# A two-layer hybrid trunk on one core: output stores and residual loads move from SyncE's queue to GpSimd's, and the sums of weights are issued earlier

## The chip, the core and the metric

The kernel runs on one core of a Trainium2 chip. The core has five engines that each work through a queue of their own: TensorE (PE, matrix products), VectorE (DVE), ScalarE (ACT), GpSimd (POOL) and SyncE (SP, which here only issues DMA transfers). ACT and GpSimd can issue DMA transfers too. Sixteen DMA engines move the data. The metric is the time of one execution in microseconds (us); less is better. A row of a view names the line of kernel.py (L115 is line 115), the engine, the operation and its operands by the program's names (out<-in).

## The reference

The input has 512 tokens of width 1024, to which 16 learned meta tokens are prepended, 528 positions in all. Two layers (DEPTH is 2) do the following, in fp32, and the meta positions are dropped at the end:

```python
for l in range(DEPTH):
    h = rmsnorm(h_res, norm_gain[l])
    proj = h @ w_in[l]
    u_pool, z_pool, c_q, c_kv, k_rope, z_mla, g_pool, g_mla = jnp.split(proj, IN_SPLIT_POINTS, axis=-1)
    y_pool = (pool_mix(u_pool, pool_w_group[l], pool_scale[l]) * jax.nn.silu(z_pool)) @ pool_w_up[l]
    o_mla = mla(c_q, c_kv, k_rope, pos, ...)
    y_mla = (o_mla * jax.nn.silu(z_mla)) @ mla_w_up[l]
    merged = jax.nn.sigmoid(g_pool) * y_pool + jax.nn.sigmoid(g_mla) * y_mla
    h_res = h_res + merged @ w_out[l]
```

`mla` is causal attention with 8 heads over low-rank queries and keys, with a norm on both; `pool_mix` takes running means over windows of 2, 4, 8 and 16 positions. The last line is the one that matters here: the product with `w_out` is added to the residual stream, which the next layer reads.

## The kernel before

All activations are held transposed, as tiles of 128 features by 528 positions, and each product works on the positions in two halves of 264 (in layer 1 mostly 256). An fp32 product is made of three products at reduced precision: weights and activations are split into a high and a low part, and `mm3` (lines 187 to 193) issues high by high (L188), high by low (L191) and low by high (L192) into one accumulator.

Weights come from DRAM in chunks of 128 by 512 (256 KB). `fetch` (L115) issues the load on SP's queue into one of three buffers named `raw`; ACT makes the high part `whi` (L183) and DVE the low part `wlo` (L184). Loads are requested four chunks ahead of their use, and a load can't start until `wlo` of the chunk three before it has been made, since that frees the buffer.

Two groups of products are done by a scheme that saves multiplications and needs sums of weight chunks instead: four output tiles of the product with `w_out` (m = 3 to 6, the tuple `OUT`) in each layer, with sums named `wsum`, and the gate tiles of layer 1, with sums named `wsumgp`. The sums are made in DRAM by transfers alone. `weight_sums` yields eight small functions for each pair of weight tiles: four copies, issued by SP (L350), and four adds, issued by GpSimd (L353), which accumulate onto the copies. An issue waits for a matmul that stands a given time back in the planner's count: `behind(ins, earlier(9000))` makes a copy wait for the last `mm3` that was planned 9000 ns or more before, and an add waits for one 4000 ns back.

What sets the order: the program is written by a planner that keeps a clock `clk` of estimated matmul time. `upto(name)` runs the plan of products until the named one is done; `after(ns, fn)` calls `fn` when the clock has moved on by `ns`. In layer 0 the functions of `weight_sums` are called every 4000 ns from a point behind the product `y3` (`up("y3")`), in layer 1 every 4500 ns. On top of this a scheduler of the language sets the final order on each engine; so the program's order on an engine isn't always the order of the code.

At the end of a layer the eight mu tiles (`mu0` to `mu7`, the products with `mla_w_up`) are made, then `blend` prepares the scheme's operands, and the output tiles follow: o0, o1, o2, the four of `OUT` (`out_pairs`), then o7. For the four of `OUT`, `residual` (L1098) loads the residual into `xb` on GpSimd's queue ahead of time, and `finish` adds to it in place and stores on GpSimd's queue: to the DRAM buffer `scr` in layer 0 (L1121), to the output `yT` in layer 1. For m = 0, 1, 2 and 7, `ev_o` does all of this on SP: it loads the residual into a temporary tile when the product is done (from `scr` in layer 1, L1060; from the input `xT` in layer 0, L1063), lets DVE add (L1066), and stores from SP (`yT` at L1070, `scr` at L1072). Between mu and out in layer 0, `meta_queries` and `meta_out` handle the attention of the meta positions; lines 1011, 1013, 1027 and 1028 belong to that, and line 297 is the split of an activation into its parts.

Of the kernel before, what the change touches and what calls it, by code (L numbers as in the profile page):

```python
# [14 lines left out]
ALU = mybir.AluOpType  # L15
# [7 lines left out]
NM = 16  # L23
# [35 lines left out]
OUT = (3, 4, 5, 6)  # L59
# [13 lines left out]
def trunk(ctx, tc, xT, pos, win, wkr, wqb, wkb, wvb, wgr, wpu, wmu, wout, gains, const, yT):  # L73
    nc = tc.nc
    pe, act, dve, gp, sp = nc.tensor, nc.scalar, nc.vector, nc.gpsimd, nc.sync
# [11 lines left out]
    def nm(s):  # L87
        uid[0] += 1
        return f"{s}_{uid[0]}"
# [4 lines left out]
    def tmp(w=W):  # L94
        return tp.tile([P, w], F32, tag="tmp", name=nm("tmp"), bufs=3)
# [15 lines left out]
    xb = cp.tile([P, 8, W], F32, name="xb")  # L111
# [30 lines left out]
    def other_loads(made):  # L142
        for k, m in ((2, 0), (4, 1), (6, None)):
            ins = sp.dma_start(xb[:, k:k + 2, :T], xT[:, k:k + 2, :])
            behind(ins, made)
            if m is not None:
                raw = rawt()
                behind(sp.dma_start(raw, win[0, MT_CKV + m, :, 512:1024]), made)
                early.append(raw)
        behind(sp.dma_start(cst, const), made)  # L150
        behind(sp.dma_start(posb[:, :T], pos.partition_broadcast(P)), made)
        dve.tensor_copy(maskw[:, 512 - P:], cst[:, C_MASK:C_MASK + P])
        dve.tensor_copy(identr, ident)
# [43 lines left out]
    def earlier(ns):  # L197
        return next((m for c, m in reversed(past) if c <= clk[0] - ns), past[0][1])
# [52 lines left out]
    def step():  # L251
        c = next(main, None)
        if c is None:
            flush()
            return False
        clk[0] += c
        while pend and pend[0][0] <= clk[0]:
            pend.pop(0)[1]()
        return True

    def after(ns, fn):
        pend.append((clk[0] + ns, fn))
        pend.sort(key=lambda e: e[0])

    def ready():
        while pend and pend[0][0] <= clk[0] + 12000.0:
            pend.pop(0)[1]()
# [5 lines left out]
    def upto(name):  # L273
        while name not in done:
            if not step():
                break
# [10 lines left out]
    def fill_now(ns):  # L287
        end = clk[0] + ns
        while clk[0] < end and step():
            pass  # L290
# [9 lines left out]
    def behind(ins, other):  # L300
        tc.add_manual_dep(ins.ins, other.ins.name,
                          mybir.DependencyInfo(mybir.DependencyClass.Sync, mybir.DependencyReason.DATA))
# [24 lines left out]
    scr = dp.tile([P, 8, SEQ], F32, name="scr")  # L327
# [13 lines left out]
    def weight_sums(name, w):  # L341
        def made(u, i):
            a, b = w[2 * u], w[2 * u + 1]
            d = wsum[name][u]
            src = {0: (b[:, 0:512], b[:, 512:1024]), 2: (a[:, 0:512], b[:, 0:512]), 1: (a[:, 0:512], d[:, 0, :]),
                   3: (a[:, 512:1024], d[:, 1, :])}
            return d[:, i, :], src[i]

        def copy(d, src):
            behind(sp.dma_start(d, src[0]), earlier(9000))  # L350

        def add(d, src):
            behind(gp.dma_start(d, src[1], accum_op=ALU.add), earlier(4000))  # L353

        for u in range(len(w) // 2):
            for fn, i in ((copy, 0), (copy, 2), (add, 0), (copy, 1), (add, 2), (add, 1), (copy, 3), (add, 3)):
                yield lambda fn=fn, u=u, i=i: fn(*made(u, i))

    class Layer:
# [695 lines left out]

        def ev_o(self, m, nxt):
            def ev(ps, a, b):
                xr = tmp()
                if self.last:
                    sp.dma_start(xr[:, a:b], scr[:, m, a - NM:b - NM])  # L1060
                    xn = xr
                else:
                    sp.dma_start(xr[:, a:b], xT[:, m, a:b])  # L1063
                    nxt.xt[m] = xb[:, m]
                    xn = nxt.xt[m]
                dve.scalar_tensor_tensor(out=xn[:, a:b], in0=ps, scalar=0.5, in1=xr[:, a:b],  # L1066
                                         op0=ALU.mult, op1=ALU.add)
                a0 = max(a, NM)
                if self.last:
                    sp.dma_start(yT[:, m, a - NM:b - NM], xn[:, a:b])  # L1070
                    return
                sp.dma_start(scr[:, m, a0 - NM:b - NM], xn[:, a0:b])  # L1072
                if m == 7:
                    nxt.square_x(m)
            return ev
# [168 lines left out]
        def go(self, nxt):  # L1244
            l = self.l
            up = lambda name: upto((l, name))
            mix = iter(range(99))
            if l == 0:
                for k in range(8):
                    if k in (0, 1, 3, 5):  # L1250
                        step()
                    self.split_h(k)
                    if k == 0:
                        other_loads(first)
            up("ckv1")
            if l == 0:
                for k in range(8):
                    self.square_x(k)
            self.norm_sums()
            up("u1")  # L1260
            for m in range(2):
                self.mix(m, self.window(m))
            up("u3")
            s2 = self.window(2)
            up("k3")
            s3 = self.window(3)
            up("zp0")
            self.mix(2, s2)
            up("zp1")
            self.mix(3, s3)  # L1270
            self.k_factors()
            up("y3")
            if l == 0:
                sums = [*weight_sums(0, [wout[0, m] for m in OUT]), *weight_sums("gp", [win[1, MT_GP + m] for m in range(8)])]
                for i, fn in enumerate(sums):
                    after(4000 * (i + 1), fn)
            up("qr1")
            for s, (a, b) in enumerate(FULL):
                a0 = max(a, self.x0)
                self.stat(self.acc[:, a0:b], a0, b, C_CQ, self.acc_last)  # L1280
            up("qn3")
            self.qk_stats()
            if l == 0:
                fill_now(2600)
            kq = self.prep(0)
            if l == 1:
                for i, fn in enumerate(weight_sums(1, [wout[1, m] for m in OUT])):
                    after(4500 * (i + 1), fn)
            fill_now(2600)
            due[0] = None  # L1290
            prev = None
            for h in range(H):
                kn_ = self.head(h, kq, prev, lambda: self.mixed(next(mix)))
                self.gap()
                self.mixed(next(mix))
                if h + 1 < H:
                    kq = self.prep(h + 1)
                self.pv(prev, (2, 3))
                prev = kn_
                self.gap()  # L1300
                self.mixed(next(mix))
            fill_now(1300)
            self.pv(prev, (0, 1))
            fill_now(2600)
            if not self.last:
                self.meta_queries()
            self.pv(prev, (2, 3))
            up("gm6")
            if self.last:
                self.gates_again()  # L1310
            up("gm7")
            ready()
            if not self.last:
                for p in range(4):
                    self.meta_out(p)
            up("mu7")
            for m in OUT:
                self.residual(m)
            for k in range(4):
                fill_now(2600)  # L1320
                self.blend(k)
            up("o7")
            if nxt is not None:
                for k in range(8):
                    nxt.split_h(k)
# [76 lines left out]
```

## Time and profile before

| what | before |
|---|---|
| median of the runs (lowest, highest) | 789.2 us (788.14, 790.12) |
| the profiled execution's own time | 790.13 us |
| its span, first to last instruction | 788.4 us |
| mean granted TensorE clock in it | 0.998 |
| PE busy | 776.1 us, 98% |
| DVE busy | 592.9 us, 75% |
| ACT busy | 442.5 us, 56% |
| GpSimd busy | 212.4 us, 27% |
| moved by DMA | 109.15 MB, mean 138 GB/s |

Of the DMA engines' time, SP's queue takes 39.6% of the span (q1 in the profile) and GpSimd's 9.5% (q0). A load of a `raw` chunk lands some 3 us after its issue in the median. "Busy" counts time in which an engine works on an instruction; issuing a DMA counts on GpSimd (0.5 to 0.9 us each), and is shown on SP as its queue (SPq). In a list of waits, "PE mm L188 <- ACT q L297: 1.9, 1, 1.9" reads: PE's instructions of line 188 stood for 1.9 us in total, once, 1.9 us at most, until ACT's instruction of line 297 that wrote q had finished. The granted clock is the share of full TensorE speed that the chip allowed in a stretch.

### The profile page before, as it was taken

How to read it: one execution, taken by the hardware profiler on the slowest of the kernel's cores; microseconds unless marked ns; L12 is line 12 of the kernel's file. 1: busy time of each engine (PE TensorE's matmuls, PEld its weight loads, DVE VectorE, ACT ScalarE, POOL GpSimd, SP SyncE). 2: the span in 40 equal slices, each digit the busy share in tenths (PEclk: the TensorE clock that was granted, in tenths of full speed). 3: DMA queues.
4: the chain of work that ended last, by engine and by line, in shares of the span. 5: the costliest groups of instructions: out<-in, count | busy, mean ns of one | idle time of the engine just before them, and what ended most of it. 6: DMA issues, size and time to landing. Idle time of an engine off the chain costs nothing.

```text
span 788.4 us, 15369 instructions
## 1 busy us (share of the span) xinstructions
PE 776.1 (98%) x5493; PEld 713.6 (91%) x5493; DVE 592.9 (75%) x1329; ACT 442.5 (56%) x1007; POOL 212.4 (27%) x291
## 2 busy tenths in 40 slices
PE   8999999999999999999999999999999999999998
PEld 8999899999999999899997898887788899888888
DVE  5847788447779987589875487775998899874995
ACT  7645656635656565544564356555657676754451
POOL 1034504103343352101110145131015325440101
PEclk9999999999999999999999999999999999999999
DMA  6242334764556355658732422435356566664552
GB/s 242 81 101 83 99 120 130 180 161 129 132 139 140 102 129 154 137 166 191 224 122 93 96 87 80 133 94 167 114 146 150 165 169 168 156 208 133 163 173 81
DMA packets 65196, 109.15 MB, mean 138 GB/s; under 512 B 10448, under 2 KB 16976, under 8 KB 65120
## 3 DMA queue, kind: packets, MB, share of 16 engines
q1 hardware_dynamic: 58096, 93.72, 39.6%
q0 software_dynamic: 6016, 12.62, 9.5%
q10 hardware_dynamic: 1008, 1.84, 0.6%
q8 instruction: 43, 0.70, 0.4%
q14 instruction: 33, 0.27, 0.1%
HBM read 100.18 MB, written 22.62 MB: 156 GB/s over the span
## 4 chain that ended last, share of the span: by engine, by line
PE 89%; DMA 4%; DVE 3%; issue 2%; ACT 2%; POOL 0%; ACTq 0%; DVEq 0%; POOLq 0%
PE mm L188 26%; PE mm L192 26%; PE mm L191 25%; PE mm L946 2%; PE S L191 2%; PE S L188 2%; PE S L192 2%; DMA raw<-win 1%; DVE wlo L184 1%; PE o L952 1%; PE o L951 1%; DMA raw<-wout 1%; PE S L500 1%; ACT whi L183 1%; DMA xb<-xT 1%
## 5 line engine op out<-in xcount | busy, mean ns | idle before, releaser
L188 PE MATMUL mm<-hh,whi 128*128 128x264 f32 (+2 forms) x1000 | 306.9, 310 | 1.0 <-DVE u L543 0.3
L191 PE MATMUL mm<-hl,whi 128*128 128x264 f32 (+2 forms) x1000 | 305.4, 307 | 0.0
L192 PE MATMUL mm<-hh,wlo 128*128 128x264 f32 (+2 forms) x1000 | 304.9, 308 | 0.2 <-DVE wlo L184 0.2
L184 DVE TENSOR_TENSOR wlo<-raw,whi 128x512 fp32r<-128x512 f32 (+2 forms) x261 | 188.6, 727 | 98.5 <-ACT whi L183 91.6
L183 ACT ACTIVATE whi<-raw 128x512 fp32r<-128x512 f32 (+2 forms) x261 | 156.3, 602 | 164.4 <-PE mm L191 83.5
L188 PEld LDWEIGHTS mm<-hh,whi 128*128 128x128 f32 x1000 | 187.5, 188 | 12.2 <-ACT whi L183 1.4
L191 PEld LDWEIGHTS mm<-hl,whi 128*128 128x128 f32 x1000 | 188.1, 188 | 8.7
L192 PEld LDWEIGHTS mm<-hh,wlo 128*128 128x128 f32 x1000 | 187.2, 188 | 8.9 <-DVE wlo L184 0.8
L188 PE MATMUL mm<-cq,whi 128*128 128x264 f32 (+2 forms) x156 | 48.6, 312 | 0.9 <-ACT whi L183 0.9
L192 PE MATMUL mm<-cq,wlo 128*128 128x264 f32 (+2 forms) x156 | 48.0, 310 | 0.6 <-DVE wlo L184 0.6
L702 POOL TENSOR_TENSOR racc<-racc,tmp 128x264 f32<-128x264 f32 (+1 forms) x15 | 14.2, 950 | 111.5 <-ACT tmp L701 87.5
L191 PE MATMUL mm<-cq,whi 128*128 128x264 f32 (+2 forms) x140 | 43.4, 311 | 0.0
L879 DVE CUSTOM_DVE_ANT_0 S<-S,maskw,nqs 128x288 f32<-128x288 f32 (+4 forms) x80 | 38.3, 495 | 2.5 <-PE S L192 2.2
L188 PE MATMUL mm<-u,whi 128*128 128x264 f32 (+1 forms) x108 | 35.2, 326 | 0.0
L298 DVE TENSOR_TENSOR tl<-mm,th 128x512 fp32r<-128x512 f32 (+1 forms) x64 | 29.2, 480 | 7.6 <-ACT th L297 6.3
L192 PE MATMUL mm<-u,wlo 128*128 128x264 f32 (+1 forms) x108 | 34.8, 322 | 0.0
L850 POOL TENSOR_TENSOR tmp<-kp,bc 64x528 f32<-64x528 f32 x16 | 25.8, 1613 | 29.8 <-DVE xb L651 11.4
L886 ACT ACTIVATE cq<-S,bia 128x400 f32<-128x400 f32 (+2 forms) x48 | 24.6, 516 | 14.6 <-DVE bia L914 8.8
L926 POOL TENSOR_TENSOR cq<-cq,rs 128x384 f32<-128x384 f32 (+1 forms) x32 | 32.4, 1012 | 0.0
L188 PE MATMUL mm<-q,whi 128*128 128x264 f32 (+1 forms) x96 | 30.5, 329 | 1.9 <-ACT q L297 1.9
L188 PEld LDWEIGHTS mm<-cq,whi 128*128 128x128 f32 x156 | 29.4, 188 | 2.6 <-ACT whi L183 1.1
L192 PEld LDWEIGHTS mm<-cq,wlo 128*128 128x128 f32 x156 | 29.3, 188 | 2.6 <-DVE wlo L184 1.1
(341 smaller groups left out, 1659.8 us busy)
## 6 DMA issues: line engine op xcount, KB each, us to landing
raw<-win SPq DMA_DIRECT2D x139, 256.0 KB, 2.8
raw<-wout SPq DMA_DIRECT2D x22, 256.0 KB, 3.0
bc<-kdr SPq DMA_DIRECT2D x16, 264.0 KB, 4.9
wsum<-wout SPq DMA_DIRECT2D x16, 256.0 KB, 3.5
raw<-wpu SPq DMA_DIRECT2D x16, 256.0 KB, 3.4
wsumgp<-win SPq DMA_DIRECT2D x16, 256.0 KB, 3.3
raw<-wmu SPq DMA_DIRECT2D x16, 256.0 KB, 3.1
raw<-wsumgp SPq DMA_DIRECT2D x16, 256.0 KB, 3.2
```

The source lines that it names most:

```text
L183: act.activation(hi[:, :n], raw[:, :n], AF.Copy)
L184: dve.tensor_sub(lo[:, :n], raw[:, :n], hi[:, :n].bitcast(F32))
L188: first = pe.matmul(out, wh, xh, start=start, stop=False, skip_group_check=more)
L191: pe.matmul(out, wh, xl, start=False, stop=False, skip_group_check=more)
L192: newest[0] = pe.matmul(out, wl, xh, start=False, stop=stop, skip_group_check=more)
L298: dve.tensor_sub(lo[:, a:b], src, hi[:, a:b].bitcast(F32))
L702: self.acc_last = gp.tensor_add(self.acc[:, a:b], self.acc[:, a:b], t[:, :b - a])
L850: gp.tensor_mul(kf[r0:r0 + 64, :], self.kp[r0:r0 + 64, :], bc[r0:r0 + 64, :])
L879: dve.tensor_tensor_reduce(out=sv, in0=sv, in1=mask, scale=nqs[:, i, h:h + 1], scalar=3e38, op0=ALU.add, op1=ALU.min, accum_out=bia[:, c:c ...
L886: act.activation(pv, sv, AF.Exp, scale=-1.0, bias=bia[:, i:i + 1], accum_out=rs[:, c:c + 1])
L926: gp.tensor_mul(pt[i][:, NM:], pt[i][:, NM:], rs[:, i:i + 1].to_broadcast([P, n - NM]))
L946: pe.transpose(tr[:, P * (i - j):P * (i - j + 1)], pt[i][:, NM + P * j:NM + P * (j + 1)], ident)
```

## The change

There are three edits. A copy for the sums of weights now waits for a matmul 14000 ns back instead of 9000. The sums of layer 0 are called from a point ahead of `up("y3")` instead of behind it, every 3850 ns instead of 4000. And `ev_o` loads no residual any more: `residual` loads it into `xb` on GpSimd's queue for all eight tiles, DVE adds in place in `xb`, and the stores to `scr` and `yT` are issued by GpSimd, apart from the two of `yT` for m = 7, which stay on SP.

```diff
@@ weight_sums
         def copy(d, src):
-            behind(sp.dma_start(d, src[0]), earlier(9000))
+            behind(sp.dma_start(d, src[0]), earlier(14000))

@@ ev_o
             def ev(ps, a, b):
-                xr = tmp()
+                x = xb[:, m, a:b]
+                dve.scalar_tensor_tensor(out=x, in0=ps, scalar=0.5, in1=x, op0=ALU.mult, op1=ALU.add)
                 if self.last:
-                    sp.dma_start(xr[:, a:b], scr[:, m, a - NM:b - NM])
-                    xn = xr
-                else:
-                    sp.dma_start(xr[:, a:b], xT[:, m, a:b])
-                    nxt.xt[m] = xb[:, m]
-                    xn = nxt.xt[m]
-                dve.scalar_tensor_tensor(out=xn[:, a:b], in0=ps, scalar=0.5, in1=xr[:, a:b],
-                                         op0=ALU.mult, op1=ALU.add)
+                    (sp if m == 7 else gp).dma_start(yT[:, m, a - NM:b - NM], x)
+                    return
+                nxt.xt[m] = xb[:, m]
                 a0 = max(a, NM)
-                if self.last:
-                    sp.dma_start(yT[:, m, a - NM:b - NM], xn[:, a:b])
-                    return
-                sp.dma_start(scr[:, m, a0 - NM:b - NM], xn[:, a0:b])
+                gp.dma_start(scr[:, m, a0 - NM:b - NM], xb[:, m, a0:b])
                 if m == 7:
                     nxt.square_x(m)

@@ go
             self.k_factors()
-            up("y3")
             if l == 0:
                 sums = [*weight_sums(0, [wout[0, m] for m in OUT]), *weight_sums("gp", [win[1, MT_GP + m] for m in range(8)])]
                 for i, fn in enumerate(sums):
-                    after(4000 * (i + 1), fn)
+                    after(3850 * (i + 1), fn)
             up("qr1")
...
             up("mu7")
-            for m in OUT:
+            for m in (0, 1, 2, *OUT, 7):
                 self.residual(m)
```

The order of the instructions shows what moves. Names carry a running number, which differs between the two programs by a few; `wmu` is `mla_w_up`, `win` the input weights, `wout` the output weights.

On SP's queue at the end of layer 0, round the loads for the mu tiles, before:

```order
L350 DMA wsumgp_125<-win 128x512
L115 DMA raw_4789<-win 128x512
L115 DMA raw_4827<-wmu 128x512
L115 DMA raw_4890<-wmu 128x512
L350 DMA wsumgp_125<-win 128x512
L115 DMA raw_4927<-wmu 128x512
L115 DMA raw_4964<-wmu 128x512
```

and after:

```order
L350 DMA wsumgp_126<-win 128x512
L115 DMA raw_4796<-win 128x512
L350 DMA wsumgp_126<-win 128x512
L115 DMA raw_4834<-wmu 128x512
L115 DMA raw_4897<-wmu 128x512
L115 DMA raw_4934<-wmu 128x512
L115 DMA raw_4971<-wmu 128x512
```

The last copies (of the fourth and last group, 126) have moved ahead of the mu tiles' loads; before, copies of the third group (125) stood there and the last copy stood among the loads for the output tiles.

On GpSimd's queue at the end of layer 0, before:

```order
L353 DMA wsumgp_125<-win 128x512 x2
L353 DMA wsumgp_125<-wsumgp_125 128x512 x2
L1098 DMA xb<-xT 128x528 x2
L353 DMA wsumgp_126<-win 128x512
L1098 DMA xb<-xT 128x528 x2
L353 DMA wsumgp_126<-win 128x512
L353 DMA wsumgp_126<-wsumgp_126 128x512 x2
L1121 DMA scr<-xb 128x248 x2
```

and after (where residual's load is line 1091 and `ev_o`'s store is line 1065):

```order
L353 DMA wsumgp_126<-win 128x512 x2
L353 DMA wsumgp_126<-wsumgp_126 128x512
L1091 DMA xb<-xT 128x528 x2
L353 DMA wsumgp_126<-wsumgp_126 128x512
L1091 DMA xb<-xT 128x528 x6
L1065 DMA scr<-xb 128x248
L1065 DMA scr<-xb 128x264
```

The adds of the last group now stand ahead of the residual loads but for one, there are eight residual loads instead of four, and stores of `ev_o` follow.

On SP's queue in layer 1, in the stretch of the heads, before:

```order
L860 DMA qhl_106<-q_1349_7237 32x512
L115 DMA raw_8297<-win 128x512
L350 DMA wsum_130<-wout 128x512
L115 DMA raw_8341<-win 128x512
L840 DMA bc_8491<-kdr_122 128x528
L115 DMA raw_8370<-wsumgp_123 128x512
L115 DMA raw_8414<-win 128x512
L115 DMA raw_8436<-win 128x512
L350 DMA wsum_130<-wout 128x512
```

and after:

```order
L860 DMA qhl_106<-q_1341_7225 32x512
L350 DMA wsum_130<-wout 128x512
L115 DMA raw_8285<-win 128x512
L350 DMA wsum_130<-wout 128x512
L115 DMA raw_8329<-win 128x512
L840 DMA bc_8479<-kdr_122 128x528
L115 DMA raw_8358<-wsumgp_123 128x512
L115 DMA raw_8402<-win 128x512
```

The two copies shown stand one load and three loads further ahead in the queue than before.

## The prediction

> **What bounds the kernel now.** I read the head of the page first, then the waits of TensorE (PE), then the chain of waits with a table of windows round the largest wait.
>
> ```profile
> span 788.4 us, 15369 instructions
> PE 776.1 (98%) x5493; PEld 713.6 (91%) x5493; DVE 592.9 (75%) x1329; ACT 442.5 (56%) x1007; POOL 212.4 (27%) x291
> ...
> PE mm L188 <- ACT q L297: 1.9, 1, 1.9
> PE mm L188 <- ACT whi L183: 1.2, 2, 0.9
> ...
> PE mm L192 <- DVE wlo L184: 0.8, 2, 0.6
> ...
> PE S L188 <- ACT sv L1142: 0.3, 1, 0.3
> ```
>
> PE is busy for 98% of the span, and the change removes no matmul. So it can save only what PE loses: its waits (in the waits: us in total, times, longest), and time at a lower clock. The largest wait is one of 1.9 us for ACT's q of line 297. The chain of waits (start, duration, what) shows what led to it, at the step that makes the first mu tile:
>
> ```profile
> 333.00 0.68 DVE wlo L184
> ...
> 334.64 0.21 ACT q L297
> 334.89 0.51 PE mm L188 x2
> ```
>
> PE starts at 334.89 after its wait of 1.9, so it stopped near 333.0. Between the two rows shown stand three short steps of DVE and ACT (lines 1013, 1027, 1028); all of them queue behind the split of a weight chunk into whi (ACT) and wlo (DVE), and that split came late. ACT's row says that it stood for 2.67 us until the chunk's load had landed; the load and the answer on its landing are the next two lines, then a later load of the same kind, which landed in 2.7 us; then the two GpSimd DMAs (POOL) round these, and the window after the gap.
>
> ```profile
> 331.72 1.16 ACT L183 ACTIVATE whi<-raw 128x512 fp32r<-128x512 f32 x2 [2.67 <-DMA raw<-wmu]
> 327.24 0.93 SPq L115 DMA_DIRECT2D raw<-wmu  x2
> DMA to landing us min/median/max: 4.4/4.4/4.4
> DMA to landing us min/median/max: 2.7/2.7/2.7
> 325.62 0.81 POOL L353 DMA_DIRECT2D wsumgp<-win  x1 [9.25 <-PE mm L192]
> 334.01 0.82 POOL L353 DMA_DIRECT2D wsumgp<-wsumgp  x1 [5.02 <-DMA wsumgp<-wsumgp]
> 335.50:339.00 3.50, 3.50 (x19) 3.50 (x18) 2.21 (x8) 1.27 (x4) 0.00 (x0) 0.51 0.65 154
> ```
>
> In the window's line PE's busy time comes second and the granted clock third from the end: PE is busy for all 3.5 us, at a clock of 0.51. At half clock some 3.4 us do the work of 1.7. So this place costs 1.9 + 1.7 = 3.6 us, and the wait in it comes from the late load.
>
> **The change part by part.** The profiled execution took 790.13 us, 1.7 more than its span; the three runs shown have a median of 789.2, 0.9 below it, and a lowest of 788.14. I make the sum against 790.13.
>
> (a) The gap at 333. In the built program the add (line 353) issued at 325.62 now waits for an earlier matmul, and it has been issued before the chunk's load leaves SP; the next add is tied to the matmul of this row, so it can't start before 327.75:
>
> ```profile
> 327.47 0.28 PE L192 MATMUL mm<-hh,wlo 128*128 128x264 f32 x1
> ```
>
> An add moves 256 KB both ways beside the load. Before, the add of 325.62 was in flight when the load left at 327.24; now none is, and the next follow about 0.9 us later. The load that landed in 2.7 us had an add 0.3 us behind it (at 334.01, the load at 333.71), so I take 2.7 for 4.4. All steps behind it then come 1.7 us sooner, and I let 1.6 of it reach PE: −1.6. Bounds: 0 (the load is as late as before) and −1.9 (no gap).
>
> (b) The half clock after it. The gap is the only stop of PE near it. With 0.3 us left of it I take the half clock as gone: −1.7, bounds 0 and −1.7.
>
> [...]
>
> (c) The end of layer 0. SP's rows there: the stores and residual loads that leave this queue, a copy that now goes 55 us earlier, and the load behind them, which the chain of waits then follows to PE:
>
> ```profile
> 368.88 0.96 SPq L1063 DMA_DIRECT2D tmp<-xT  x2
> 369.94 0.50 SPq L350 DMA_DIRECT2D wsumgp<-win  x1
> 370.54 0.53 SPq L115 DMA_DIRECT2D raw<-wout  x1
> 370.54 6.70 DMA raw<-wout
> ...
> 381.04 0.39 PE S L188
> ```
>
> The load took 6.70 us beside the copy and the two residual loads. Without them it lands some 3 us sooner, but PE loses only 0.3 here (S <- sv in its waits). So −0.3, bounds 0 and −0.4.
>
> (d) Layer 1, at 644. Another late load, 6.08 us in flight, had a copy 1.8 us ahead of it:
>
> ```profile
> 635.35 0.52 SPq L350 DMA_DIRECT2D wsum<-wout  x1
> 637.17 6.08 DMA raw<-win
> ```
>
> That copy now starts near 629. PE's waits there are part of 1.2 (whi) and 0.8 (wlo), about 0.5 us: −0.4, bounds 0 and −0.5.
>
> (e) Layer 1, at 617: here the same edit makes a load later. A copy was issued at 612.72. The next, which came 7 us after the load of 616.99, is now tied to a matmul that ended at 614.65, so it goes just ahead of the load of 616.99, beside an add:
>
> ```profile
> 614.37 0.28 PE L192 MATMUL mm<-hh,wlo 128*128 128x256 f32 x1
> 612.72 0.52 SPq L350 DMA_DIRECT2D wsum<-wout  x1
> 616.36 0.84 POOL L353 DMA_DIRECT2D wsum<-wsum  x1
> 616.99 4.73 DMA raw<-win
> ...
> 629.10 0.35 DVE tmp L637
> ```
>
> From this load the chain of waits runs by whi, wlo and DVE's queue to tmp at 629.10, which PE takes at once. The nearest row for "copy, add, load" is a load at 297.04, with a copy 2.2 us and an add 0.6 us ahead:
>
> ```profile
> 294.83 0.52 SPq L350 DMA_DIRECT2D wsumgp<-win  x1
> 296.41 0.79 POOL L353 DMA_DIRECT2D wsumgp<-wsumgp  x1
> DMA to landing us min/median/max: 6.0/6.0/6.0
> ```
>
> 6.0 for 4.7 is 1.3 us later, and I let 1.2 reach PE: +1.2, bounds 0 and +1.6 (the 6.7 of (c) less 4.7, less 0.4 of cover that ACT and DVE may have).
>
> (f) Copies of layer 0 from line 350 come about 25 to 55 us earlier. From 150 to 330 us each chunk is split 4 to 9 us before its first matmul, so SP's waits on ties there cost PE nothing. From 85 to 150 it is tighter; the first copy, at 120.3 before, may now go at 91.4. One copy falls ahead of the load of 107.56, whose chunk is split about 1 us before PE wants it: I take +0.2, bounds 0 and +1.0.
>
> (g) GpSimd's 19 new DMAs: 8 residual loads, 8 scr stores, 3 yT stores. What they cost the issuing engine, and how such transfers landed from either queue (KB each, median us to landing):
>
> ```profile
> L1121 POOL DMA_DIRECT2D scr<-xb x8 | 4.4, 554 | 18.9 <-DVE xb L1116 18.9
> scr<-xb SPq DMA_DIRECT2D x4, 124.0 KB, 5.7
> scr<-xb POOLq DMA_DIRECT2D x4, 124.0 KB, 2.4
> xb<-xT POOLq DMA_DIRECT2D x4, 264.0 KB, 5.3
> tmp<-xT SPq DMA_DIRECT2D x8, 132.0 KB, 3.1
> ```
>
> 19 × 0.55 us is 10.5 us of an engine that is busy for 212 of 788 us and idle for most of the end of each layer: 0. Behind these issues on its queue stand only the last adds and the other stores. Should that cover go, a store or a preload is late by its 0.55 us; the preloaded residuals have some 10 us before they are used, so the 2.2 us by which 5.3 exceeds 3.1 doesn't show either. On DVE the edit in place replaces one operation by one of the same shape: 0. The preload fills xb's own rows, so no buffer is added to wait for.
>
> [...]
>
> Sum: −1.6 − 1.7 − 0.3 − 0.4 + 1.2 + 0.2 = −2.6, so 787.5 us.
>
> **The rivals.** *More late loads vanish and (e) doesn't bite.* For: (c) and (d) show loads that took 6 us and more wherever a copy stood ahead. Against: PE's other waits, 4 us in all, stand mostly at steps without a load. With (a), (c), (d) at their best ends and (e), (f) at 0: −1.9 − 1.7 − 0.4 − 0.5 = −4.5, 785.6 us.
>
> *The change does nothing at 333.* Two adds now come within 2 us of the load instead of one on either side; if the traffic as a whole sets the landing, it stays at 4.4 and (a), (b) are 0: +0.7, 790.8 us.
>
> *The half clock stays without the gap.* The gap is 1.92 us and no other row shows how short a stop is enough, so a clock that falls on its own schedule isn't excluded: (b) = 0, −0.9, 789.2 us. [...]
>
> *Slower: the early sums starve the stretch from 106 to 150.* PE has no wait there now, but its loads are the tightest of layer 0:
>
> ```profile
> 125.00:150.00 25.00, 25.00 (x208) 25.00 (x207) 17.10 (x33) 15.16 (x39) 11.42 (x13) 1.00 0.64 162
> 147.90 0.63 ACT L183 ACTIVATE whi<-raw 128x512 fp32r<-128x512 f32 x1 [2.23 <-DMA raw<-wpu]
> 149.83 0.28 PE L188 MATMUL mm<-u,whi 128*128 128x264 f32 x1
> ```
>
> This chunk is ready at 148.53 and used at 149.83, 1.3 us of cover, and ACT waits for its load. More copies and adds now run beside such loads. By (e)'s row a load between copy and add lands 3.3 us later than one at 2.7; less 1.3 of cover that is 2 us, and with the chain behind it I say 2.2. One such chunk eats the gain, two give −2.6 + 4.4, 791.9 us. Against: copies stood at 120 to 146 us already, and PE never waited.
>
> **How the numbers follow.** 0.3% of 789.2 is 2.4 us, about what a measurement can tell here: faster is below 786.8, slower above 791.6. Chances: the forecast 0.42 (787.5, own range 786.0 to 788.9 by the middle of the bounds of (a) to (f)), of which I put 0.18 below 786.8; more loads 0.20 (785.6); nothing at 333 0.12 (790.8); half clock stays 0.10 (789.2); starved 0.16 (791.9). Faster 0.20 + 0.18 = 0.38; same 0.24 + 0.12 + 0.10 = 0.46; slower 0.16. The range from 785.2 to 791.2 leaves out the starved case and little else.
>
> **What the profile after would show.** (a) The chunk's load near 327 lands in 2.7 to 3.2 us, and PE's wait on q of line 297 is under 0.5. (b) No window under 0.9 clock behind it. (c) wout's load at the end of layer 0 lands in about 4 us and PE's wait on sv is gone. (d) No PE wait on wlo near 644. (e) The load at about 614 to 617 lands in 6 us and PE waits about 1.3 us near 629. (f) No PE wait from 85 to 330. (g) POOL's busy time grows by about 10 us and no PE wait names line 926 in layer 0. The prediction is wrong if PE waits for whi or wlo before 150, or if the q wait stays near 1.9.

## The result and the profile after

The changed kernel takes 785.44 us (median of 7 runs, 783.7 to 786.4), the kernel before 788.76 in 7 runs beside it (786.87 to 790.12): ratio 0.9956, 95% interval 0.9941 to 0.9971. Run again beside later experiments it gave 0.9952 (0.9936 to 0.9968). So it is faster by 0.3 to 0.6%. Its time lies below the forecast of 787.5 and near the lower end of the range of 785.2 to 791.2. The profiled execution took 785.38 us.

The head of the page after, and PE's waits (us in total, times, longest):

```profile
span 783.4 us, 15391 instructions
PE 774.6 (99%) x5493; PEld 712.5 (91%) x5493; DVE 592.2 (76%) x1329; ACT 443.6 (57%) x1007; POOL 222.5 (28%) x310
...
PE mm L188 <- ACT whi L183: 1.1, 2, 0.9
...
PE mm L192 <- DVE wlo L184: 0.8, 2, 0.6
PE mm L188 <- DVE tmp L637: 0.6, 1, 0.6
```

Of the 1.9 us on q of line 297, 0.1 is left, and the wait on sv of line 1142 is gone. GpSimd is busy 10.1 us longer. The wait on tmp of line 637 has grown from 0.1 to 0.6. PE's total on whi looks unchanged (1.2 before, 1.1 now), and 0.9 of it stand near the end in both (761 us before, 756 now); but the other 0.3 stood at 6 us before and stand at 113 us now.

The place of the first mu tile, in the timeline after: the load (three in one row, from 325.84; the one that matters is the second, whose landing is the next line), the split on ACT, the two adds on GpSimd, and a window over the 3.5 us from 333:

```profile
325.84 3.10 SPq L115 DMA_DIRECT2D raw<-wmu  x3
DMA to landing us min/median/max: 2.6/2.6/2.6
330.71 1.15 ACT L183 ACTIVATE whi<-raw 128x512 fp32r<-128x512 f32 x2 [0.90 <-DMA raw<-wmu]
328.92 0.82 POOL L353 DMA_DIRECT2D wsumgp<-win  x1 [8.75 <-PE mm L192]
329.49 1.11 POOL L353 DMA_DIRECT2D wsumgp<-wsumgp  x1
333.00:336.50 3.50, 3.36 (x28) 3.15 (x27) 3.50 (x13) 2.42 (x8) 0.00 (x0) 1.00 0.93 236
```

The load was issued at 328.01 and landed in 2.6 us; the adds start 0.9 and 1.5 us behind it. ACT waits 0.90 where it waited 2.67, PE is busy for 3.36 of 3.50 us, and the clock in the third column from the end is 1.00.

The matmuls of the program take the same time in both traces (a mean of 289, 285 and 286 ns in each for the 728 of 128x264 with hh or hl at lines 188, 191 and 192, and of 395 to 397 ns for the 200 of 128x512). So the place where time is won or lost can be read from the starts of matmuls that both have: the table gives, in us, how much longer or shorter a stretch of PE's stream (named by its time in the trace of before) took than in the one trace of before. The other columns are the experiments below; each is one profiled execution.

| stretch of before | after | after, again | sums sooner | GpSimd | copies 14000 | sums + copies | one add | layer 1 copies | one copy back | later start | few ties | few ties, GpSimd |
|---|---|---|---|---|---|---|---|---|---|---|---|---|
| 103 to 150 | +1.3 | +0.8 | +1.4 | 0 | 0 | +1.0 | 0 | 0 | +0.3 | 0 | 0 | 0 |
| 150 to 155 | 0 | 0 | +1.7 | 0 | 0 | 0 | 0 | 0 | 0 | 0 | 0 | 0 |
| 332 to 335, the gap | −1.8 | −1.8 | −1.9 | +0.2 | −0.3 | −1.8 | −1.7 | 0 | −1.7 | +0.8 | −1.8 | −1.8 |
| 335 to 339, the clock | −1.5 | −1.6 | −1.6 | −1.6 | −1.6 | −1.5 | −1.6 | −1.6 | −1.5 | −0.6 | −1.5 | −1.5 |
| 380 to 382 | −0.5 | −0.5 | −0.5 | −0.5 | −0.5 | −0.5 | −0.2 | +0.2 | −0.5 | −0.5 | +0.7 | −0.5 |
| 453 to 458 | −0.6 | −0.6 | −0.3 | −0.4 | 0 | −0.2 | −0.5 | −0.6 | −0.6 | −0.6 | −0.2 | −0.6 |
| 593 to 598 | −1.1 | −0.8 | −0.1 | +0.2 | −1.1 | −1.1 | +0.3 | −1.1 | −1.1 | −1.1 | −1.1 | −1.1 |
| 616 to 618 | −0.9 | 0 | 0 | 0 | 0 | 0 | 0 | 0 | 0 | −0.9 | 0 | −0.9 |
| 628 to 630 | +0.5 | +0.2 | +0.1 | 0 | +0.5 | +0.5 | −0.2 | +0.3 | 0 | +0.5 | 0 | −0.1 |
| 643 to 646 | −0.4 | −0.4 | +0.4 | +0.1 | −0.4 | −0.4 | 0 | −0.4 | −0.4 | −0.4 | −0.4 | −0.4 |

The first 60 us scatter by some 2 us between executions and the stretch from 646 to 700 by 1.5, and the rows at 453 and at 616 follow no edit: 616 differs between two executions of the changed kernel itself. These are told of no further, but for 616 under (e) below. The later start has a half clock of its own (0.71 from 337.00 to 340.50 of its trace, and a mean of 0.998 over the execution, as in before); its row shows a shift of it and not a gain.

### The profile page after: what moved, and what is told of

Its sections match the earlier page's. It is cut to its first block, busy times and chain, and to the rows that moved or that the text cites. A ratio compares the mean times of both kernels' runs of the same rounds, so it can differ in the third digit from the quotient of the medians.

```text
span 783.4 us, 15391 instructions
## 1 busy us (share of the span) xinstructions
PE 774.6 (99%) x5493; PEld 712.5 (91%) x5493; DVE 592.2 (76%) x1329; ACT 443.6 (57%) x1007; POOL 222.5 (28%) x310
## 4 chain that ended last, share of the span: by engine, by line
PE 86%; DVE 5%; DMA 5%; issue 2%; ACT 1%; POOL 0%; ACTq 0%; DVEq 0%
PE mm L188 25%; PE mm L192 24%; PE mm L191 24%; PE S L191 2%; PE S L192 2%; PE S L188 2%; PE mm L946 2%; DVE wlo L184 2%; PE o L952 1%; PE o L951 1%; DMA raw<-wsumgp 1%; PE S L500 1%; DMA raw<-win 1%; PE mm L402 1%; DMA wsum<-wsum 1%
## 5 line engine op out<-in xcount | busy, mean ns | idle before, releaser
L353 POOL DMA_DIRECT2D wsum<-wout x8 | 6.9, 863 | 89.2 <-PE mm L192 83.8
L924 POOL TENSOR_TENSOR pm<-pa,rs 128x16 f32<-128x16 f32 x32 | 11.4, 357 | 70.6 <-DVE rs L919 64.8
```

The source lines that it names most:

```text
L924: gp.tensor_mul(self.pm[:, i, 16 * odd:16 * odd + 16], pt[i][:, 0:NM], rs[:, i:i + 1].to_broadcast([P, NM]))
```

## The experiments

**The three edits apart.** First the edit on the sums of layer 0 alone:

```diff
             self.k_factors()
-            up("y3")
             if l == 0:
...
-                    after(4000 * (i + 1), fn)
+                    after(3850 * (i + 1), fn)
```

> The kernel before, with one of the three edits: the sums of layer 0 are called ahead of up("y3") and every 3850 ns; copies stay tied 9000 ns back, and SP keeps the stores and residual loads of ev_o. Theory A (the gain is the late mu load, freed by the earlier add): PE's wait on q of line 297 goes from 1.9 to under 0.5 us, no half clock behind it, and the time is about 3 us below the kernel before (ratio 0.996). Rival B (the gain comes from SP's queue being freed of stores and residual loads): wait and half clock stay and the time is within 1 us of before. Rival C (the gain comes from the copies tied to older matmuls): as B.

Measured: ratio 0.9999 (0.9984 to 1.0015), no gain. The gap at mu0 went as theory A said, but the sum doesn't: 3.1 us came back between 103 and 155 us, which is the mechanism of the rival "the early sums starve the stretch". In its timeline, SP's loads and a copy, the add on GpSimd, the landing of the second of the loads from 146.32, and what ACT and PE made of it:

```profile
145.63 0.52 SPq L350 DMA_DIRECT2D wsum<-wout  x1
146.32 1.02 SPq L115 DMA_DIRECT2D raw<-wpu  x2
145.47 0.84 POOL L353 DMA_DIRECT2D wsum<-wout  x1 [5.94 <-PE mm L192]
DMA to landing us min/median/max: 7.7/7.7/7.7
154.19 0.63 ACT L183 ACTIVATE whi<-raw 128x512 fp32r<-128x512 f32 x1 [4.81 <-DMA raw<-wpu]
155.52 0.39 PE L188 MATMUL mm<-u,whi 128*128 128x264 f32 x1 [0.89 <-ACT sq L783]
```

A copy and an add went out within 0.2 us of each other, the load beside them took 7.7 us, and PE stood. So theory A named the right place and missed what else the edit does.

Second, the residual loads and stores of `ev_o` on GpSimd alone (the diff of `ev_o` and of the line with `residual`):

> The kernel before, with one of the three edits: residual loads of all eight output tiles and the stores of ev_o on GpSimd; sums as before. Theory A: the wait of 1.9 us on q of line 297 stays, PE's wait on sv at the end of layer 0 shrinks by 0.3 us or less, and the time is within 1 us of before. Rival B: 2 to 4 us below before.

Measured: ratio 0.9994 (0.9974 to 1.0013). The wait on q was 2.1 us, the wait on sv gone. Rival B falls. Its window behind the gap has a lesson of its own:

```profile
PE mm L188 <- ACT q L297: 2.1, 1, 2.1
335.50:339.00 3.50, 3.50 (x32) 3.50 (x31) 2.32 (x8) 1.33 (x5) 0.00 (x0) 1.00 0.76 164
```

The gap is as long as before, and the clock stayed at 1.00, with 32 matmul rows where there were 19. So a gap of 2 us doesn't always bring the half clock.

Third, the older tie alone:

```diff
-            behind(sp.dma_start(d, src[0]), earlier(9000))
+            behind(sp.dma_start(d, src[0]), earlier(14000))
```

> The kernel before, with one of the three edits: copies tied 14000 ns back instead of 9000, sums of layer 0 called where they were. Theory A: the q wait stays at 1.9 us; in layer 1 the wait on wlo near 644 us loses 0.4 us and PE waits 0.5 to 1.2 us near 629 us, so the time is within 1 us of before. Rival C: 2 to 4 us below before, with the waits at 596 and 617 us gone.

Measured: ratio 0.9981 (0.9965 to 0.9997), some 1.5 us. The q wait is 1.6 us. In layer 1 the terms of 629 and 644 came, and a gain of 1.1 us at 596 with them, which theory A didn't have and rival C did; 617 stayed.

Both edits on the sums, without the move to GpSimd:

> The two edits on the sums together, without the move to GpSimd. Theory A: about as fast as the changed kernel (785.4) but for 0.3 us at the end of layer 0; a load near 107 us lands in 6 us beside the first copy and PE waits about 1 us for whi near 113 us, which the kernel with the sums called sooner alone does not show, since its first copy comes later. Rival B: slower than the changed kernel by 2 us or more.

Measured: ratio 0.9961 (0.9947 to 0.9976), the whole gain within the interval. The load near 107 (106.31 there) landed in 5.1 us, not 6, and PE lost nothing at 113: its loss came in two parts, 0.3 at 103.5 us and 0.7 at 118.6. Theory A was wrong there, and in that the sums called sooner alone would not lose near 113 (PE waits 0.7 us for whi at 114.4). Alone the two edits make 0.9999 and 0.9981; together they make more, because the older tie takes most of the 3.1 us back that the early sums cost alone (+1.0 instead, in one execution).

**One add.** Is it the add beside the load that makes the gap?

```diff
-        def add(d, src):
-            behind(gp.dma_start(d, src[1], accum_op=ALU.add), earlier(4000))
+        def add(d, src, ns=4000):
+            behind(gp.dma_start(d, src[1], accum_op=ALU.add), earlier(ns))
...
-                yield lambda fn=fn, u=u, i=i: fn(*made(u, i))
+                yield lambda fn=fn, u=u, i=i: fn(*made(u, i), *([14000] if (name, fn, u, i) == ("gp", add, 2, 2) else []))
```

> The kernel before, with a single add (GpSimd's second of the third group of wsumgp, issued at 325.62 us there) tied 14000 ns back instead of 4000; nothing else changes. Theory A (this add beside the mu load makes the load late): the load near 327 lands in about 2.7 us instead of 4.4, PE's wait on q of line 297 falls from 1.9 to under 0.5 us, no waits appear elsewhere, and the time is about 2 us lower, with few runs below full clock. Rival D (the copies and the traffic as a whole make it late): load and wait stay within 0.4 us of before.

Measured: ratio 0.9973 (0.9960 to 0.9985), 2.7 us between the medians, for one transfer that starts some 10 us sooner. Its adds, the landing of the load issued at 328.04, and PE's wait:

```profile
316.43 1.13 POOL L353 DMA_DIRECT2D wsumgp<-win  x1
328.96 0.86 POOL L353 DMA_DIRECT2D wsumgp<-wsumgp  x1 [11.40 <-PE mm L192]
DMA to landing us min/median/max: 2.7/2.7/2.7
PE mm L188 <- ACT q L297: 0.2, 1, 0.2
```

Theory A stands for the gap, D falls: the copies there were those of before.

**Layer 1's copies alone.**

```diff
-            behind(sp.dma_start(d, src[0]), earlier(9000))
+            behind(sp.dma_start(d, src[0]), earlier(14000 if name == 1 else 9000))
```

> The kernel before, with the copies of layer 1 alone tied 14000 ns back. Theory E (a copy and an add issued together delay the loads behind them by 2 us and more, and the older tie separates them): the waits of PE on pa of line 926 near 596 us (0.7 to 0.9 us in before) go, the wait near 644 shrinks by 0.4, one of 0.5 us appears near 629; the q wait at 334 stays; together about 1 us less. Rival (execution scatter): the waits at 596 stay.

Measured: ratio 0.9977 (0.9962 to 0.9992). The q wait stayed at 1.9; −1.1 us at 593 to 598 and −0.4 at 643 came, so scatter falls as the reason for 596. In the trace of before, SP and GpSimd at 582 us, PE's wait of the heads, how that add and that copy landed, the landing of the load that SP issued next (at 586.73), and GpSimd's first step of the head that PE then waited for:

```profile
582.21 0.51 SPq L350 DMA_DIRECT2D wsum<-wout  x1
581.86 0.88 POOL L353 DMA_DIRECT2D wsum<-wout  x1 [46.28 <-PE mm L192]
PE mm L946 <- POOL pa L926: 0.8, 2, 0.4
DMA to landing us min/median/max: 7.7/7.7/7.8
DMA to landing us min/median/max: 5.4/5.4/5.4
594.72 1.12 POOL L924 TENSOR_TENSOR pm<-pa,rs 128x16 f32<-128x16 f32 x1 [2.30 <-DVE rs L919]
```

The same rows with layer 1's copies alone moved (the load is the first of the three issued from 584.28):

```profile
576.44 0.50 SPq L350 DMA_DIRECT2D wsum<-wout  x1
579.42 0.87 POOL L353 DMA_DIRECT2D wsum<-wout  x1 [46.27 <-PE mm L192]
DMA to landing us min/median/max: 4.0/4.0/4.0
591.31 0.52 POOL L924 TENSOR_TENSOR pm<-pa,rs 128x16 f32<-128x16 f32 x1 [1.33 <-DVE rs L919]
```

The copy left the add's company, the load landed in 4.0 us instead of 5.4, and GpSimd waited 1.33 us for DVE's rs instead of 2.30. That the load's delay reaches rs by way of DVE's queue (wlo stands ahead of rs) is read from the order of the rows, not tried apart.

**One copy back.** The changed kernel, where one copy of layer 1 (the second of its second group) has its old tie:

```diff
-        def copy(d, src):
-            behind(sp.dma_start(d, src[0]), earlier(14000))
+        def copy(d, src, ns=14000):
+            behind(sp.dma_start(d, src[0]), earlier(ns))
...
+                fn(*made(u, i), *([9000] if (name, fn, u, i) == (1, copy, 1, 2) else []))
```

> The changed kernel, with one copy of layer 1 (the second of its second group) tied 9000 ns back again. Theory: the wait on tmp of line 637 near 624 us (0.6) falls to 0.1 to 0.2, all else as in the changed kernel, so about 0.5 us less, which is inside the scatter of the runs. If the place at 611 (where only the changed kernel lacks a wait on tmp of line 967) shows 0.6 us of wait again, that one was scatter or hung on this copy.

Measured, in four runs: ratio 0.9954 (0.9937 to 0.9971), no difference that can be measured from the changed kernel. The wait on tmp of line 637 fell from 0.6 to 0.2 and the stretch lost its +0.5: this copy is the cause there. With layer 0 the same program as in the changed kernel, the stretch from 103 to 150 lost 0.3 instead of 1.3: that cost varies from one execution to the next.

**A later start, a shorter step.** The changed kernel with `up("y3")` back ahead of the sums and 3400 ns between them:

> The changed kernel, with the sums of layer 0 called behind up("y3") again, as before, and every 3400 ns, so that the last ones come as early as in the changed kernel, but the first copy some 20 us later. Theory F (the early copies near 105 us collide with the loads there and cost 1.3 us): PE's wait on whi near 113 us is gone, the q wait stays under 0.5 us, and the time is about 1 us below the changed kernel. Rival: the denser sums make other loads of layer 0 late and PE waits 1 us or more between 130 and 330 us.

Measured: ratio 0.9978 (0.9964 to 0.9993), slower than the changed kernel. Theory F holds for the place it names (0 from 103 to 150), yet the new step put an add just ahead of the mu tiles' loads. GpSimd's add, SP's loads, the first one's landing, PE's wait and the window behind it:

```profile
325.46 0.81 POOL L353 DMA_DIRECT2D wsumgp<-win  x1 [8.55 <-PE mm L999]
326.35 3.10 SPq L115 DMA_DIRECT2D raw<-wmu  x3
DMA to landing us min/median/max: 6.7/6.7/6.7
PE mm L188 <- ACT q L297: 2.7, 1, 2.7
337.00:340.50 3.50, 3.50 (x21) 3.50 (x22) 2.81 (x11) 1.83 (x6) 0.00 (x0) 0.71 0.61 158
```

An add 0.9 us ahead of the load: 6.7 us to landing, and the gap is longer than ever. It is the counterpart of the experiment with one add.

**Few ties.** If ties alone make the gain, they can be set without calling the sums sooner: the kernel before, with the one add tied 14000 ns back, and layer 1's copies tied 14000 ns back but for the one of the last but one experiment.

```diff
-        def copy(d, src):
-            behind(sp.dma_start(d, src[0]), earlier(9000))
+        def copy(d, src, ns=14000 if name == 1 else 9000):
+            behind(sp.dma_start(d, src[0]), earlier(ns))
...
-            behind(gp.dma_start(d, src[1], accum_op=ALU.add), earlier(4000))
+            behind(gp.dma_start(d, src[1], accum_op=ALU.add), earlier(ns))
...
+        far = {("gp", add, 2, 2): (14000,), (1, copy, 1, 2): (9000,)}
...
+                yield lambda fn=fn, u=u, i=i: fn(*made(u, i), *(far.get((name, fn, u, i), ())))
```

> The kernel before, with ties alone changed: the one add of the third group of wsumgp tied 14000 ns back, the copies of layer 1 tied 14000 ns back but for the second of the second group (9000). The sums of layer 0 are called as before, and SP keeps the stores and residual loads. By the sites measured so far: −1.7 at mu0, −0.5 for the half clock in a mean over runs, −1.1 at 596, −0.4 at 644, 0 at 629, 0 near 113; sum −3.7, as fast as the changed kernel or up to 0.5 us faster, ratio to before about 0.995. If the changed kernel draws a further gain from SP's freed queue, this one is slower than it by more than 0.5 us.

Measured: ratio 0.9955 (0.9938 to 0.9973), the changed kernel's own value, with SP's queue as it was. The same ties with the move to GpSimd:

> The same ties, with residual loads and stores of ev_o on GpSimd as in the changed kernel. Theory: −0.5 more at the end of layer 0 (PE's wait on sv), else the same; ratio about 0.9945. Rival: the move itself costs or gains nothing that shows.

Measured: ratio 0.9942 (0.9922 to 0.9963). The −0.5 at the end of layer 0 came (with SP's stores that stretch gave −0.5 to +0.7 from kernel to kernel, +0.7 in the one just told of; what sets it is under (c) below). And beside them the changed kernel:

> The changed kernel once more, beside the other two on the same chip. Theory: ratio 0.9955 to before again; PE's wait near 113 us (1.3 in its first profile, 0.2 in the same code of the kernel with one copy back) is between these, and the place near 611 us has a wait on tmp of line 967 again.

Measured: ratio 0.9952 (0.9936 to 0.9968). The version with few ties and the move is 0.1% below it; the intervals overlap for the most part, so it isn't shown to be faster.

**How often the clock halves.** Every run lists its mean granted clock, though not where it fell. In the two profiled executions with a half clock inside the program the mean is 0.998, in the eleven others 0.999 or 1. Of 83 runs of the kernel before on the three chips of these experiments, 32 had 0.998 or less; their mean time is 790.8 us, that of the other 51 is 789.3. Of the kernels that kept a gap of 1.6 to 2.7 us at mu0, 20 of 44 runs had 0.998 or less (8 of 10 with the gap of 2.7). Of the kernels without that gap, 4 of 75 had it: none of 53 runs of the changed kernel, both edits on the sums, one copy back and the two with few ties, 2 of 12 with the sums called sooner alone (PE stops twice within 1 us near 155 us there) and 2 of 10 with one add moved.

The traces show that the length of the stop alone doesn't settle it. The rows cut PE's time: the stop in before and the half clock that follows it, then the stop with GpSimd, the stop with the later start, and the 30 us round the stop with copies 14000:

```profile
332.11:335.52 3.41, 1.49 (x12) 1.28 (x11) 3.10 (x11) 1.93 (x6) 0.82 (x1) 1.00 0.52 129
335.52:338.94 3.42, 3.42 (x17) 3.42 (x17) 2.19 (x8) 1.27 (x4) 0.00 (x0) 0.50 0.64 151
332.50:335.50 3.00, 0.94 (x8) 0.72 (x7) 2.97 (x10) 1.56 (x5) 0.82 (x1) 1.00 0.42 135
334.00:337.00 3.00, 0.27 (x4) 0.06 (x2) 2.49 (x7) 1.56 (x6) 0.00 (x0) 1.00 0.85 124
330.00:360.00 30.00, 28.36 (x232) 28.10 (x232) 25.46 (x56) 12.72 (x25) 4.02 (x6) 1.00 0.71 183
```

PE is idle for 1.92 us of the first row (3.41 less 1.49), and the clock is 0.50 over the 3.4 us of the second. PE is idle for 2.06 us with GpSimd, where the clock stayed at 1.00 behind the stop; for 2.73 us with the later start, where it was 0.71 from 337.00 to 340.50; and for 1.64 us with copies 14000, where it stayed at 1.00. So 1.92 us of idle PE went with a half clock in one execution and 2.06 us without one in another. Over the runs it came more often with the gap of 2.7 (8 of 10) than in before, with 1.9 in its one trace (32 of 83). What decides it in a single execution isn't shown. Copies 14000 had it in 5 of 12 runs; whether its stop is longer in those isn't on record.

## Why the prediction was right or wrong

*(a), the gap: right.* −1.8 for −1.6, by the mechanism named: one add that starts sooner takes the wait away (0.2 us is left of 1.9), and one put 0.9 us ahead of the load makes it longer (2.7 us).

*(b), the half clock: the cause right, the size wrong.* The sum took 1.7 from the profiled execution of before, which had the half clock; most runs don't. It comes with the gap in 32 of 83 runs and costs 790.8 − 789.3 = 1.5 us there, so 0.6 us in a mean run. The rival "the half clock stays without the gap" falls: 4 of 75 runs against 52 of 127 with the gap. Nor does the gap bring it each time: in the traces it came behind 1.92 and 2.73 us of idle PE and not behind 2.06 and 1.64, and no run shows what decides.

*(c), the end of layer 0: the size right, the cause only in part.* −0.5 for −0.3; each of the three edits alone brought it in its one execution. The prediction put the load's 6.70 us down to the copy and the two residual loads ahead of it. It had overlooked an add of GpSimd that left 0.02 us behind that copy:

```profile
369.96 0.82 POOL L353 DMA_DIRECT2D wsumgp<-wsumgp  x1 [3.89 <-PE mm L192]
```

With the sums called sooner alone, the copy and the add are gone from there while SP's stores and residual loads stay, and the load (369.72 there) landed in 3.1 us. Where the pair stayed (one add, layer 1's copies, few ties), the load took 6.0, 6.9 and 6.6 us and the stretch came out at −0.2, +0.2 and +0.7. So the copy and the add made this load late, and not the transfers that move to GpSimd. Moving those alone helped as well, since the copy then left 1.1 us ahead of the add (367.40 and 368.53), with the load between them.

*(d), at 644: right,* −0.4 for −0.4, by layer 1's copies. The 0.1 on whi went with it; the 0.2 on wlo, which was to go too, stayed.

*(e), at 617 to 629: direction right, size wrong.* +0.2 to +0.5 for +1.2. The step that failed is the row it was measured by, a load that landed in 6.0 us. The order that it foresaw came in the second execution of the changed kernel (SP's copy and load, GpSimd's add, the landing of the load):

```profile
611.19 0.51 SPq L350 DMA_DIRECT2D wsum<-wout  x1
613.51 0.34 SPq L115 DMA_DIRECT2D raw<-win  x1
612.88 0.83 POOL L353 DMA_DIRECT2D wsum<-wsum  x1
DMA to landing us min/median/max: 5.0/5.0/5.0
```

With the copy 2.3 us and the add 0.6 us ahead, the load landed in 5.0 us, where it took 4.7 before with the add alone. With copies 14000 and with both edits on the sums the order was the same: 5.3 and 5.6 us to landing, and PE lost 0.6 and 0.9 from 618 to 630. In the first execution of the changed kernel the order was another:

```profile
609.86 0.51 SPq L350 DMA_DIRECT2D wsum<-wout  x1
611.02 0.34 SPq L115 DMA_DIRECT2D raw<-win  x1
DMA to landing us min/median/max: 3.1/3.1/3.1
```

The copy stood 1.2 us ahead, but the add came 1.1 us behind the load (at 612.12) and not ahead of it, and the load landed in 3.1 us. There the next load but one (614.30, landed in 6.3 us) came late; whether it carries the +0.5 wasn't tried. The row at 616 goes with this order: its −0.9 stands in the three executions in which the load left ahead of the add, and in no other.

*(f), the early copies: wrong size.* +0.2 was taken, with +1.0 as the bound; +0.3, +0.8 and +1.3 came in three executions of that code. PE's wait for whi at 113 us is one of the two signs by which the prediction said it would be wrong. The place was right in part: of the +1.3, 0.5 came at 113.5 us, where PE waits for this load's whi, and 0.3 just behind it. The rows after show the copy, SP's broadcasts of kdr, the load, its landing and ACT's wait for it:

```profile
104.53 0.50 SPq L350 DMA_DIRECT2D wsum<-wout  x1
105.89 0.79 SPq L840 DMA_DIRECT2D bc<-kdr  x2
106.79 0.36 SPq L115 DMA_DIRECT2D raw<-win  x1
DMA to landing us min/median/max: 6.0/6.0/6.0
112.87 0.63 ACT L183 ACTIVATE whi<-raw 128x512 fp32r<-128x512 f32 x1 [4.65 <-DMA raw<-win]
```

The load stood behind the broadcasts before, too, and landed in 4.0 us; with a copy ahead of both it lands in 6.0 us, and the term had been taken as nearly covered. The other 0.4 of the +1.3 came at 103.5 us, where PE waits for kt of line 309. The chain of waits there leads back to a small transfer of SP (ksr, at 92.00), which left 1.1 us behind a copy and took 2.98 us; whether the copy made it late wasn't tried apart. The rival "starved" is what happens with the sums called sooner alone (3.1 us back), not with the whole change.

*(g), GpSimd's issues: right.* 10.1 us more busy time, no wait, 0.9994 for the move alone.

*What the sum lacked* is the term that made it too small: −0.8 to −1.1 at 596. The edit of (d) and (e) takes a third copy of layer 1, at 582.21, away from an add. I had priced the copies whose loads PE waited for directly; here PE waited for GpSimd's line 926, the wait of 0.8 us in total that the waits of before list, and the late load stood two engines ahead of it.

Put together from the runs: −1.8 (a), −0.6 (b), −0.5 (c), −0.4 (d), −1.0 (596), +0.4 (e), +0.8 (f) make −3.1 us against the runs of before, where 788.76 − 785.44 = 3.3 was measured. The prediction's −2.6 stood against a profiled execution that was 1.4 us slower than the median of all 7 runs, and which had the half clock. That −2.6 stands so near −3.1 is in part luck: (b) saved 1.1 too much and (f) cost 0.6 too little, while (e) cost 0.8 too much and the 1.0 at 596 was missing. The forecast's own range, 786.0 to 788.9, does not follow from its terms (halfway from each term to its bounds gives 786.6 to 790.1), and the measured time lies below both. It is nearest to the rival "more late loads vanish and (e) doesn't bite" (785.6), which had a chance of 0.20, and that is in part what happened, at 596.

## What to carry to other kernels

When PE is 98% busy, list each place where it waits and follow it back to the load that was late, even when the wait names another engine; then ask which other transfer shared the time of that load, and move that transfer by a few microseconds. One add moved by some 10 us made about three fifths of this gain by the ratios (0.9973 of 0.9956), while calling all the sums sooner gained nothing until the copies moved too: a shift of many transfers makes new collisions (3.1 us came back between 103 and 155 us here), so look at each load with little slack that they now pass. And don't count a half clock from one profiled execution in full; see in how many runs the clock fell (32 of 83 here).

## What was not expected of the hardware

A copy and an add of 256 KB that start within 0.4 us of each other took 7.7 to 7.8 us each at 582 us in the kernel before, where a copy took 3.3 to 3.5 in the median and an add 5.6; loads beside such a pair took 5.4 to 7.7 us, where loads of the same weights (win, wout, wpu) took 2.8 to 3.4 in the median of before. Not every such pair is slow: at 265 us in before the copy landed in 3.3 us and the add in 5.6. A load of wmu that an add left 0.9 us ahead of landed in 6.7 us, and two that an add left 0.9 us behind landed in 2.6 and 2.7, where 3.1 is the median in before. And a stop of PE of about 2 us went with a half clock in some executions and not in others: 1.92 us of idle PE came ahead of one of 3.4 us in before, and 2.06 us ahead of none with GpSimd alone.
